# Convolution stretches and bias tables in other steps of an input projection

## The chip, the cores and the metric

The kernel runs on one core of one Trainium2 chip. The metric is the device time of one execution in microseconds (us). TensorE (PE) multiplies matrices and transposes, VectorE (DVE) and ScalarE (ACT) work on tiles in SBUF and PSUM, GpSimd (POOL) on tiles in SBUF, and SyncE (SP) issues nearly all transfers.

## The reference, cut to what matters

One block of a diffusion backbone on 2048 latent and 256 context tokens of 1024 channels, all in float32. The part that the change touches is the input projection and what is made from its output:

```python
hx = modulate(rms_norm(x, norm1_g[i]), sh1, sc1)
qx, kx, vx, ux = split_proj(hx @ w_in[i])          # 512 + 512 + 512 + 1024 columns
qx_rot = axial_rope(qx, row_pos, col_pos)
kx_rot = axial_rope(kx, row_pos, col_pos)
attn_x = neighbourhood_attention(qx_rot, qx, kx_rot, vx, kc, vc, rpb[i])   # bias from rpb
conv_x = conformer_conv(ux, ...)                   # a * sigmoid(b), width 31, LayerNorm, silu
x_new = x + g1 * (jnp.concatenate([attn_x, conv_x], axis=-1) @ w_out[i])   # then the MLP
```

The vectors sh1, sc1, g1, ... come from `silu(c) @ w_ada + b_ada`.

## The kernel before, in words

Every float32 product is made of three matmuls on a high and a low part of each operand (mm3, L89 to L92). The program runs through a start, the input projection (56 to 665 us), attention, the output projection and the MLP; only the input projection is touched.

**Steps.** The 2048 tokens are two blocks of 1024, each of two halves of 512. For each block there are ten groups of 256 columns of the weight: four gated groups (u), two q, two k and two v. A step is one group on one half, 40 steps in all: block 0 has steps 0 to 19 (u 0 to 7, q 8 to 11, k 12 to 15, v 16 to 19), block 1 steps 20 to 39 in the same manner. Within a group the halves follow each other, but the first two u groups of a block are interleaved, as are the v groups of block 1. In each step TensorE fills one piece of PSUM (pt); ScalarE, VectorE and GpSimd then make what is stored: h_d from u (sg, L724 and L725), rotated and split q and k (rope_store, L576 on, with products by the cosine and sine tables), v (L613 on).

**PSUM.** It is cut into four pieces of 1024 columns, given out in turn by psA (L54). During the input projection the convolution holds one of them (pcv, L416), so three rotate.

**Convolution.** It goes in 21 stretches of 98 rows (class Conv): load (cw from h_d, L425), split (ScalarE L428, VectorE L429), fwd (three matmuls into pcv, the product cy on VectorE at L435, its high part cyh on ScalarE at L438, the low part cyl on VectorE at L439), inv one step later (six matmuls, LayerNorm on VectorE, L448 to L452) and turn another step later (four transposes L458, ScalarE L460, store L462). cy is a tile in SBUF. A counter, cv_pos, says which stretch stands where: the stretches start with the last u step of a block and one enters per step, in steps 7 to 16 and 27 to 37. The load of the next stretch is issued at the end of a step.

**Beside it.** norm_half scales the four x tiles of a half on VectorE (L218) and shifts them on GpSimd (L221). The relative-position bias is built in four parts: bias_start and bias_end (step 6), bias_head (steps 8 to 15; tables tb, a mask add on GpSimd at L287, stores to tf_d and ti_d), and bias_rows (groups 9 to 12; twelve DRAM-to-DRAM copies into bias_d, L304). ada_chunk makes the gate vectors from the weight rows wr (L490, L506); its finish (L511 on) does two matmuls (L514), loads the row of b_ada (br, L517) and adds it (L518).

The order on each engine is that of a scheduler from these calls; the SP queue issues transfers in the order that `order` prints.

Of the kernel before, what the change touches and what calls it, by code (L numbers as in the profile page):

```python
# [18 lines left out]
P = 128  # L19
D = 1024  # L20
# [21 lines left out]
def hybrid_layer(ctx: ExitStack, tc: tile.TileContext, a: dict, out: bass.AP):  # L42
# [375 lines left out]
    class Conv:  # L418
# [12 lines left out]
        def fwd(self):  # L431
            i, hl, o = self.i, cvc["hl"], cvc["ps"][:, 0:512]
            mm3(o, hl[:, 0, 0:P], hl[:, 1, 0:P], self.w[:, 1, :], self.w[:, 0, :], True, True)
            y = pa.tile([P, 2, 512], F32, tag="acc", bufs=2, name=f"cy{i}")
            VE.tensor_tensor(y, o.unsqueeze(1).broadcast_to([P, 2, 512]), cvc["ab"], ALU.mult)  # L435
            self.yh = pa.tile([P, 2, 512], F32R, tag="H", bufs=3, name=f"cyh{i}")
            self.yl = pa.tile([P, 2, 512], F32R, tag="H", bufs=3, name=f"cyl{i}")
            SE.copy(self.yh, y)  # L438
            VE.tensor_tensor(self.yl, y, f(self.yh), ALU.subtract)  # L439
# [22 lines left out]
            SY.dma_start(cv_d[:, :, self.t0:self.t0 + self.n].rearrange("k p n -> p k n"), cx[:, :, 0:self.n])  # L462

    cvs = [Conv(i) for i in range(NCB)]
    cv_pos = [0]

    def conv_at(d, last):
        i = cv_pos[0] - d  # L470
        if 0 <= i < last and not hasattr(cvs[i], f"did{d}"):
            setattr(cvs[i], f"did{d}", True)
            (Conv.inv, Conv.turn)[d - 1](cvs[i])

    def conv_end(last):
        i = cv_pos[0]
        if i < last:
            cvs[i].split()
            cvs[i].fwd()
            if i + 1 < last:  # L480
                cvs[i + 1].load()
        cv_pos[0] += 1

    def ada_chunk(ch):
        box = {}

        def load(i):
            n, k = i // KD, i % KD
            r = pa.tile([P, 512], F32, tag="wr", bufs=2, name=f"wr{ch}_{i}")
            SY.dma_start(r, wada[k * P:(k + 1) * P, ch * D + n * 512:ch * D + (n + 1) * 512])  # L490
            box[i] = r

        def step(i):
            if i == 0:
                box["a"] = pa.tile([P, D], F32, tag="ada", bufs=1, name=f"ada{ch}")
                load(0)
                return
            if i < 2 * KD:
                load(i)
            r = box.pop(i - 1)  # L500
            n, k = (i - 1) // KD, (i - 1) % KD
            acc = box["a"][:, n * 512:(n + 1) * 512]
            if k == 0:
                VE.tensor_scalar(acc, r, sil[:, 0:1], None, ALU.mult)
            else:
                VE.scalar_tensor_tensor(acc, r, sil[:, k:k + 1], acc, ALU.mult, ALU.add)  # L506
            if i == 2 * KD:
                pe_todo.append(finish)

        def finish():  # L510
            acc = box["a"]  # L511
            pg = psA(f"pg{ch}")
            for n in range(2):
                TE.matmul(pg[0:1, n * 512:(n + 1) * 512], ones[:, 0:1], acc[:, n * 512:(n + 1) * 512],  # L514
                          start=True, stop=True)
            br = pa.tile([1, D], F32, tag="m1", bufs=2, name=f"br{ch}")
            SY.dma_start(br, a["b_ada"][:, ch * D:(ch + 1) * D])  # L517
            VE.tensor_tensor(br, pg[0:1, :], br, ALU.add)  # L518
            row = {2: 0, 4: 1, 3: 2}[ch]
            if ch == 4:  # L520
                gr = gtile([1, D], F32, "gr")
                SY.dma_start(gr, a["norm2_g"])
                VE.scalar_tensor_tensor(br, br, 1.0, gr, ALU.add, ALU.mult)
            SY.dma_start(g_d[row:row + 1, :], br)
        return [(0.6, lambda i=i: step(i)) for i in range(2 * KD + 1)]
# [19 lines left out]
    def norm_half(tiles, b, hf):  # L545
        scale, shift = norm_mod(tiles, Ar, Br, f"n{b}{hf}")
        for i in range(4):
            scale(i)
            shift(i)
        return tiles  # L550

    def trans_half(tiles, b, hf, which=range(4)):
# [124 lines left out]
    first_x(3)  # L677
    mix0 = Mix(0, lambda nm: gtile([P, 1024], F32, nm), None)
    NG = len(groups)
    CB0 = (BLK - P + PAD) // CL + 1  # L680
    CBS = (CB0, NCB)
    BR0 = 9
    adas = {ch: ada_chunk(ch) for ch in (2, 3, 4)}
    G0 = NG // NB
    ADA = {G0 - 1: 2, G0: 3, G0 + 2: 4}
    RATE = {"u": (5.2, 6), "q": (5.2, 4), "k": (5.2, 4), "v": (5.2, 6)}
    xt1 = xd = None
# [22 lines left out]
    def half(gi, hf):  # L710
        b, kind, idx, _ = groups[gi]
        wget = wgets[gi]
        thv, tlv = TH[hf] if TH[hf] else (None, None)
        if kind == "u":
            ct = idx
            pt = psA(f"pu{b}{ct}{hf}")
            for t in range(4):
                for k in range(KD):
                    wh, wl = wget(k, slice(0, 2 * P))
                    sl = slice(t * P, (t + 1) * P)  # L720
                    mm3(pt[:, t * 256:(t + 1) * 256], thv[:, k, sl], tlv[:, k, sl], wh, wl, k == 0, k == KD - 1)
            sg = gtile([P, 4, P], F32, f"sg{b}{ct}{hf}")
            p4 = pt.rearrange("p (t j c) -> p t j c", t=4, j=2)
            SE.activation(sg, p4[:, :, 1, :], AF.Sigmoid)  # L724
            VE.tensor_tensor(sg, p4[:, :, 0, :], sg, ALU.mult)  # L725
            t0 = PAD + b * BLK + hf * 512
            SY.dma_start(h_d[t0:t0 + 512, ct * P:(ct + 1) * P].rearrange("(t p) c -> p t c", p=P), sg)
            if ct == 3 and hf == 1:
                cv_pos[0] = (0, CB0)[b]
                cvs[cv_pos[0]].load()  # L730
                conv_end(CBS[b])
        elif kind in "qk":
            pt = psA(f"p{kind}{b}{idx}{hf}")
            for j in range(2):
                conv_at(2 - j, CBS[b])
                for k in range(KD):
                    lh, ll = wget(k, slice(j * P, (j + 1) * P))
                    mm3(pt[:, j * 512:(j + 1) * 512], lh, ll, thv[:, k, :], tlv[:, k, :], k == 0, k == KD - 1)
            rope_store(b, kind, idx, hf, pt)
            conv_end(CBS[b])  # L740
        else:
            for t2 in range(2):
                def getter(tt, thv=thv, tlv=tlv):
                    sl = slice(tt * P, (tt + 1) * P)
                    return lambda k: (thv[:, k, sl], tlv[:, k, sl])
                row = (b * BLK + hf * 512 + t2 * 256) // W
                conv_at(2 - t2, CBS[b])
                if idx == 1 and hf == 1 and b + 1 < NB:
                    trans_half(pend["x"], b + 1, 0, (2 * t2, 2 * t2 + 1))
                v_tiles([getter(2 * t2), getter(2 * t2 + 1)], row, wget, idx, f"{b}{idx}{hf}{t2}")  # L750
            conv_end(CBS[b])
        if gi == 1 and hf == 0:
            trans_half(xt1, 0, 1)
            in_order(n_start, (VE.engine, SE.engine, GE.engine))
        if kind == "v" and idx == 1 and b + 1 < NB and hf == 1:
            TH[1] = None
            pend["x"] = x_half(b + 1, 1)
        if b > 0 and kind == "u" and idx == 0 and hf == 0:
            norm_half(pend["x"], b, 1)
        if b + 1 < NB and kind == "q" and idx == 1 and hf == 0:  # L760
            norm_half(pend["x"], b + 1, 0)
        if b > 0 and kind == "u" and idx == 1 and hf == 0:
            trans_half(pend.pop("x"), b, 1)
        if gi == 0 and hf == 1:

            ts_ = []
            for i in range(2):
                xt = x_tile(f"xc{i}")
                SY.dma_start(xt, cin[i * P:(i + 1) * P, :])
                ts_.append(xt)  # L770
            scale, shift = norm_mod(ts_, Ac, Bc, "nc")
            for i in range(2):
                scale(i)
                shift(i)
                SY.dma_start(xc_d[i * P:(i + 1) * P, :], ts_[i])
        if gi == 3 and hf == 0:
            bias_start()
            bias_end()
        if 4 <= gi < 8:
            bias_head((gi - 4) * 2 + hf)  # L780
        if gi == 1 and hf == 1:
            conv_loads()
        if gi == 2 and hf == 1:
            conv_tables()
        if hf == 0 and BR0 <= gi < BR0 + 4:
            bias_rows(gi - BR0)
        todo, pe_todo[:] = list(pe_later), list(pe_todo)
        pe_later[:], pe_todo[:] = list(pe_todo), []
        for fn in todo:
            fn()  # L790
        if kind == "v" and idx == 1 and b + 1 < NB:
            pass
        else:
            pump(*RATE[kind])
# [61 lines left out]

    steps[-4:] = [(NG - 2, 0), (NG - 1, 0), (NG - 2, 1), (NG - 1, 1)]
    for i, (gi, hf) in enumerate(steps):

        for nxt, nh in steps[i + 1:i + 3]:  # L860
            if nh == 0 and nxt not in wgets and len(wgets) < 2:
# [747 lines left out]
```

## Time and profile before

| what | us |
|---|---|
| median of 3 runs | 2565.85 |
| lowest, highest | 2565.72, 2567.3 |
| profiled execution | 2570.69 |
| its span | 2568.9 |
| TensorE busy in the span | 2430.5 (95%) |
| VectorE, GpSimd, ScalarE busy | 1790.2, 1467.8, 1248.7 |

The rows in the section below come from the profiled execution. TensorE is the engine that is nearly always at work; a wait counts for the time where it makes TensorE stand still. A row of waits names the waiting engine and line, what it waited for, the sum in us, how often, and the longest one. The granted clock (PEclk) is a share of TensorE's full speed: 1.00 is 2.4 GHz, 0.50 is 1.2 GHz.

### The profile page before, as it was taken

To read this page: it belongs to the slowest core of one execution; us is meant where nothing else is said; L and a number is where in the kernel's file an instruction comes from. 1 tells how busy PE (TensorE), PEld (TensorE's weight loads), DVE (VectorE), ACT (ScalarE), POOL (GpSimd) and SP (SyncE) were. 2 spreads that over 40 slices of the span, in tenths; PEclk is the share of its full clock that TensorE was granted. 3 is DMA by queue.
4 is the path that set the end of the run, shared out by engine and by line. 5 is a ranking of instruction groups with operands and counts; after the bars stand their busy time and mean duration, and the time that the engine had idled before them with its cause. 6 is when DMAs were issued, how large, how long until landed. Compare 5 with 4: busy or idle time off the path is not lost.

```text
span 2568.9 us, 42313 instructions
## 1 busy us (share of the span) xinstructions
PE 2430.5 (95%) x15903; PEld 2216.9 (86%) x15903; DVE 1790.2 (70%) x2465; ACT 1248.7 (49%) x2162; POOL 1467.8 (57%) x1055
## 2 busy tenths in 40 slices
PE   7997989899889999988999999999999999999997
PEld 5985889689889999987998889999889998799996
DVE  6646743666689976468666697666786676876676
ACT  4334531443689963134444554444554445454442
POOL 3537422442578856457555676555675556755564
PEclk9998999999999999999999999999999999999999
DMA  8555764653899865665333443333343334433321
GB/s 299 158 168 163 223 216 130 196 154 110 227 253 262 241 182 174 195 231 165 99 99 107 129 139 111 101 105 99 121 148 101 99 99 126 137 107 100 105 92 57
DMA packets 293882, 387.26 MB, mean 151 GB/s; under 512 B 38021, under 2 KB 231228, under 8 KB 293644
## 3 DMA queue, kind: packets, MB, share of 16 engines
q1 hardware_dynamic: 293660, 384.54, 49.7%
q8 instruction: 125, 2.05, 0.3%
q14 instruction: 81, 0.66, 0.1%
q10 hardware_dynamic: 16, 0.00, 0.0%
HBM read 308.03 MB, written 86.76 MB: 154 GB/s over the span
## 4 chain that ended last, share of the span: by engine, by line
PE 62%; DVE 10%; DMA 9%; POOL 5%; issue 4%; SPq 2%; ACT 1%; DVEq 0%; POOLq 0%; ACTq 0%
PE pall L90 18%; PE pall L91 18%; PE pall L92 18%; PE pall L1105 2%; PE pall L1069 1%; PE pall L1030 1%; DVE s L1398 1%; DMA ar<-at_d 1%; DVE ac L1501 1%; DVE ac L1497 1%; PE pall L1107 1%; DVE w L1423 1%; PE pall L1032 1%; DMA cw<-h_d 1%; DMA xn_d<-xo 1%
## 5 line engine op out<-in xcount | busy, mean ns | idle before, releaser
L90 PE MATMUL pall<-w,hh 128*128 128x512 f32 x1024 | 406.0, 397 | 11.0 <-DVE ac L1497 7.2
L91 PE MATMUL pall<-w,hh 128*128 128x512 f32 x1024 | 403.0, 394 | 0.0
L92 PE MATMUL pall<-w,hl 128*128 128x512 f32 x1024 | 397.2, 392 | 0.6 <-DVE hl L1454 0.6
L1497 DVE TENSOR_TENSOR ac<-pall,ac 128x1024 f32<-128x1024 f32 x239 | 286.8, 1214 | 73.9 <-PE pall L92 73.2
L90 PEld LDWEIGHTS pall<-w,hh 128*128 128x128 f32 x1024 | 195.1, 190 | 51.6 <-issue 4.4
L92 PEld LDWEIGHTS pall<-w,hl 128*128 128x128 f32 x1024 | 193.3, 189 | 41.9 <-DVE hl L1454 2.2
L91 PEld LDWEIGHTS pall<-w,hh 128*128 128x128 f32 x1024 | 194.8, 190 | 36.4 <-issue 0.2
L1451 ACT ACTIVATE c<-c 128x512 f32<-128x512 f32 x128 | 80.9, 632 | 157.2 <-DVE c L1471 129.2
L86 POOL TENSOR_TENSOR w_0l<-w_0r,w_0h 128x1024 fp32r<-128x1024 f32 x20 | 50.7, 2537 | 172.7 <-ACT w_0h L85 152.5
L90 PE MATMUL pall<-xah,w 128*128 128x256 f32 x512 | 144.8, 284 | 4.7 <-ACT w L1392 4.7
L92 PE MATMUL pall<-xah,w 128*128 128x256 f32 x512 | 145.2, 284 | 0.0
L91 PE MATMUL pall<-xal,w 128*128 128x256 f32 x512 | 145.0, 283 | 0.0
L1454 DVE TENSOR_TENSOR hl<-c,hh 128x512 fp32r<-128x512 f32 x128 | 123.7, 967 | 15.3 <-ACT hh L1453 15.2
L1062 POOL TENSOR_SCALAR sb<-sb,ri 128x696 f32<-128x696 f32 (+1 forms) x128 | 105.6, 826 | 49.7 <-DVE ri L1057 40.7
L1044 DVE CUSTOM_DVE_ANT_0 sb<-pall,bias 128x696 f32<-128x696 f32 (+1 forms) x128 | 108.0, 845 | 6.5 <-PE pall L1032 5.9
L1052 ACT ACTIVATE sb<-sb,mn 128x696 f32<-128x696 f32 (+1 forms) x128 | 109.6, 857 | 0.6 <-DVE mn L1044 0.6
L90 PEld LDWEIGHTS pall<-xah,w 128*128 128x128 f32 x512 | 98.1, 192 | 7.5 <-ACT w L1392 4.9
L91 PEld LDWEIGHTS pall<-xal,w 128*128 128x128 f32 x512 | 98.6, 192 | 2.8
L92 PEld LDWEIGHTS pall<-xah,w 128*128 128x128 f32 x512 | 98.6, 192 | 2.1
L90 PE MATMUL pall<-xth,w 128*128 128x256 f32 x256 | 75.2, 294 | 19.1 <-DVE pu L1459 19.1
L1105 PE MATMUL pall<-pw,v 120*128 120x256 f32 (+1 forms) x480 | 90.8, 309 | 0.8 <-ACT ob L1112 0.8
L1081 DVE TENSOR_TENSOR pw<-pall,pw 120x512 fp32r<-120x512 f32 (+1 forms) x128 | 83.5, 653 | 5.1 <-ACT pw L1076 4.7
(853 smaller groups left out, 8797.0 us busy)
## 6 DMA issues: line engine op xcount, KB each, us to landing
v<-v_d SPq DMA_DIRECT2D x144, 120.0 KB
q<-q_d SPq DMA_DIRECT2D x64, 256.0 KB
wr<-in_w_ada SPq DMA_DIRECT2D x48, 256.0 KB
v_d<-vt SPq DMA_DIRECT2D x64, 160.0 KB
wa<-in_w_ada SPq DMA_DIRECT2D x8, 1024.0 KB
x<-in_x SPq DMA_DIRECT2D x16, 512.0 KB
kr<-k_d SPq DMA_DIRECT2D x32, 256.0 KB
at_d<-ao SPq DMA_DIRECT2D x32, 256.0 KB
```

The source lines that it names most:

```text
L86: (eng or GE).tensor_tensor(l, r, f(h), ALU.subtract)
L90: TE.matmul(outp, lh, rh, start=start, stop=False)
L91: TE.matmul(outp, lh, rl, start=False, stop=False)
L92: TE.matmul(outp, ll, rh, start=False, stop=stop)
L1044: VE.tensor_tensor_reduce(sb[:, c0:SE_], d["s"][:, 512 - SC0 + c0:768], bt[:, c0:SE_], -1.0, 3e38, ALU.add, ALU.min, mn)
L1052: SE.activation(pb[:, c0:SE_], pb[:, c0:SE_], AF.Exp, bias=d["mn"], scale=-1.0, accum_out=d["sm"])
L1062: GE.tensor_scalar(pb[:, c0:SE_], pb[:, c0:SE_], d["ri"], 1.0, ALU.mult, ALU.mult)
L1081: VE.tensor_tensor(pw[0:120, 0:nch, 1, :], d["tv"], f(pw)[0:120, 0:nch, 0, :], ALU.subtract)
L1105: TE.matmul(o, VT[(pr, *key)][0:n, hd, :], pw[0:n, ch, :, :], start=(ch == 0), stop=False)
L1451: SE.activation(c, c, AF.Relu)
L1454: VE.tensor_tensor(dl, cv, f(dh), ALU.subtract)
L1497: VE.tensor_tensor(ac, po_, ac, ALU.add)
```

## The change

A table, ENTER, now says which stretch enters at which step: 0 to 7 in steps 12 to 19, 8 and 9 in steps 22 and 24, and 10 to 20 in steps 27 to 37 as before. The u steps call conv_at too. cy lies in a rotating piece of PSUM instead of SBUF. bias_start and bias_end go to step 17, bias_head to steps 20 to 27, bias_rows to groups 14 to 17. The row of b_ada is loaded at the end of a chunk's steps instead of in finish, and of the last half's four x tiles two are shifted on VectorE.

```diff
-            y = pa.tile([P, 2, 512], F32, tag="acc", bufs=2, name=f"cy{i}")
+            y = psA(f"cy{i}").rearrange("p (z n) -> p z n", z=2)
...
-    def conv_at(d, last):
-        i = cv_pos[0] - d
-        if 0 <= i < last and not hasattr(cvs[i], f"did{d}"):
-            setattr(cvs[i], f"did{d}", True)
+    def conv_at(d):
+        i = ENTER.get(now[0] - d)
+        if i is not None:
             (Conv.inv, Conv.turn)[d - 1](cvs[i])
 
-    def conv_end(last):
-        i = cv_pos[0]
-        if i < last:
+    def conv_end():
+        i = ENTER.get(now[0])
+        if i is not None:
             cvs[i].split()
             cvs[i].fwd()
-            if i + 1 < last:
-                cvs[i + 1].load()
-        cv_pos[0] += 1
+        i = ENTER.get(now[0] + 1)
+        if i is not None:
+            cvs[i].load()
...
             if i == 2 * KD:
+                box["b"] = pa.tile([1, D], F32, tag="m1", bufs=2, name=f"br{ch}")
+                SY.dma_start(box["b"], a["b_ada"][:, ch * D:(ch + 1) * D])
                 pe_todo.append(finish)
...
-            br = pa.tile([1, D], F32, tag="m1", bufs=2, name=f"br{ch}")
-            SY.dma_start(br, a["b_ada"][:, ch * D:(ch + 1) * D])
+            br = box["b"]
...
-            shift(i)
+            shift(i, VE if b and hf and i % 2 else GE)
...
-    BR0 = 9
+    G0 = NG // NB
+    NS0 = 2 * G0
+
+    ENTER = {n: i for i, n in enumerate([*range(12, 20), 22, 24, *range(27, 38)])}
+    assert len(ENTER) == NCB
+    BR0 = G0 + 4
...
             for t in range(4):
+                if t % 2 == 0:
+                    conv_at(2 - t // 2)
...
-            if ct == 3 and hf == 1:
-                cv_pos[0] = (0, CB0)[b]
-                cvs[cv_pos[0]].load()
-                conv_end(CBS[b])
+            conv_end()
...
-        if gi == 3 and hf == 0:
+        if gi == G0 - 2 and hf == 1:
             bias_start()
             bias_end()
-        if 4 <= gi < 8:
-            bias_head((gi - 4) * 2 + hf)
+        if G0 <= gi < G0 + 4:
+            bias_head((gi - G0) * 2 + hf)
```

The three places on which the terms of the prediction rest, by the order of the instructions on an engine. First VectorE at the end of block 0's q steps and the start of its k steps, before (sw and m10 belong to the rotation, x are the first half's tiles of block 1, cy and cyl the convolution's):

```order
L585 STREAM_SHUFFLE sw0q_1883<-pall 128x1024
L594 TENSOR_TENSOR m10q_1884<-pall,cos_440 128x1024
L452 TENSOR_SCALAR co_1851<-co_1851,cst_1852 98x512
L218 SCALAR_TENSOR_TENSOR x_1645<-x_1645,n10ss,Ar 128x1024
...
L435 TENSOR_TENSOR cy_1922<-pall,cab 128x1024
L607 TENSOR_TENSOR ql0q_1888<-pall,qh0q_1887 128x256 x2
L439 TENSOR_TENSOR cyl_1925<-cy_1922,cyh_1924 128x1024
L585 STREAM_SHUFFLE sw0k_2022<-pall 128x1024
L588 SCALAR_TENSOR_TENSOR m10k_2023<-pall,cos_440 128x1024
```

and now:

```order
L585 STREAM_SHUFFLE sw0q_1706<-pall 128x1024
L594 TENSOR_TENSOR m10q_1707<-pall,cos_440 128x1024
L130 RECIPROCAL n10ss<-n10ss 128x4
L218 SCALAR_TENSOR_TENSOR x_1537<-x_1537,n10ss,Ar 128x1024
...
L607 TENSOR_TENSOR ql0q_1711<-pall,qh0q_1710 128x256 x2
L585 STREAM_SHUFFLE sw0k_1802<-pall 128x1024
L588 SCALAR_TENSOR_TENSOR m10k_1803<-pall,cos_440 128x1024
L435 TENSOR_TENSOR pall<-pall,cab 128x1024
L589 SCALAR_TENSOR_TENSOR sw0k_1802<-sw0k_1802,sin_441 128x1024
L439 TENSOR_TENSOR cyl_1817<-pall,cyh_1816 128x1024
```

The lines of the convolution (L452, L435, L439) are gone from beside the scales of the x tiles; the first stretch comes in the first k step, its product goes to pall (PSUM), and cyl reads it there.

SP where the copies into bias_d stand, before, in the v steps of block 0:

```order
L592 DMA k_d<-m10k_2338 128x512 x2
L635 DMA v_d<-vt_2436 40x2x512 x3
L304 DMA bias_d_81<-tf_d 16x32x320
L304 DMA bias_d_82<-ti_d 16x32x440
L304 DMA bias_d_83<-tf_d 16x32x320
L701 DMA sin_2985<-in_sin_t 128x1024
L425 DMA cw_2356<-h_d 128x512
...
L635 DMA v_d<-vt_2507 40x2x512 x4
...
L462 DMA cv_d<-ccx_2378 128x4x98
```

and now, in the second q step of block 1 (cw_4175 is the load of stretch 12; q_d takes the rotated q of the step before):

```order
L290 DMA tf_d<-tb_4019 32x600
L291 DMA ti_d<-tb_4019 32x320
L489 DMA wr_10_4030<-in_w_ada 128x512
L489 DMA wr_11_4033<-in_w_ada 128x512
L304 DMA bias_d_81<-tf_d 16x32x320
L304 DMA bias_d_82<-ti_d 16x32x440
L304 DMA bias_d_83<-tf_d 16x32x320
...
L489 DMA wr_12_4036<-in_w_ada 128x512
L425 DMA cw_4175<-h_d 128x512
L610 DMA q_d<-qh1q_4135 64x2x512 x2
```

At the "..." of the second piece stand nine more copies and nothing else; before, loads and stores stood between groups of two to four of them.

GpSimd at the second half's x tiles of block 1, before:

```order
L86 TENSOR_TENSOR w_1l<-w_1r,w_1h 128x1024
L221 TENSOR_TENSOR x_2962<-x_2962,Br 128x1024
L221 TENSOR_TENSOR x_2964<-x_2964,Br 128x1024
L221 TENSOR_TENSOR x_2966<-x_2966,Br 128x1024
L221 TENSOR_TENSOR x_2968<-x_2968,Br 128x1024
```

now:

```order
L86 TENSOR_TENSOR w_1l<-w_1r,w_1h 128x1024
L287 TENSOR_TENSOR tb_2948<-tb_2948,cm 64x600
L221 TENSOR_TENSOR x_2779<-x_2779,Br 128x1024
L221 TENSOR_TENSOR x_2783<-x_2783,Br 128x1024
L287 TENSOR_TENSOR tb_3137<-tb_3137,cm 64x600
```

and VectorE there now:

```order
L729 TENSOR_TENSOR sg_2925<-pall,sg_2925 128x512
L130 RECIPROCAL n11ss<-n11ss 128x4
L218 SCALAR_TENSOR_TENSOR x_2779<-x_2779,n11ss,Ar 128x1024
...
L218 SCALAR_TENSOR_TENSOR x_2785<-x_2785,n11ss,Ar 128x1024
L221 TENSOR_TENSOR x_2781<-x_2781,Br 128x1024
L729 TENSOR_TENSOR sg_3089<-pall,sg_3089 128x512
L221 TENSOR_TENSOR x_2785<-x_2785,Br 128x1024
L230 TENSOR_TENSOR t11l<-pall,t11h 128x8x128 x4
```

Two of the four adds of Br are on VectorE, around a product of a gated step (sg), and two table adds (L287) stand beside the other two on GpSimd.

## Rows read from the trace of the kernel before

**Rows 1.** Page, part 1: busy us, share of the span, instructions.

```profile
PE 2430.5 (95%) x15903; PEld 2216.9 (86%) x15903; DVE 1790.2 (70%) x2465; ACT 1248.7 (49%) x2162; POOL 1467.8 (57%) x1055
```

**Rows 2.** TensorE's waits, 150 to 400: us in total, times, longest.

```profile
PE pall L91 <- DVE cyl L439: 8.0, 2, 6.5
PE pall L227 <- POOL x L221: 6.3, 3, 2.8
PE pall L90 <- ACT cyh L438: 5.1, 1, 5.1
PE pall L90 <- ACT ccx L460: 3.3, 1, 3.3
PE pall L458 <- DVE cy L435: 2.3, 1, 2.3
PE pall L90 <- ACT cw L428: 1.8, 1, 1.8
...
```

**Rows 3.** Windows: us, PE busy, granted clock, DMA share, GB/s.

```profile
203.10:206.50 3.40, 3.40 (x9) 0.50 0.75 161
237.20:257.70 20.50, 8.90 (x21) 0.50 0.60 171
377.10:387.40 10.30, 8.02 (x37) 0.50 0.09 25
496.60:503.40 6.80, 3.73 (x9) 0.50 0.82 261
```

**Rows 4.** TensorE's waits, 440 to 660.

```profile
PE pall L90 <- DVE br L518: 5.3, 1, 5.3
PE pall L90 <- ACT ccx L460: 3.9, 2, 2.0
PE pall L91 <- DVE cyl L439: 2.4, 2, 1.2
PE pall L90 <- ACT cyh L438: 1.9, 2, 1.0
PE pall L458 <- DVE cy L435: 1.6, 1, 1.6
```

**Rows 5.** Lines L439 and L435: duration ns min/median/max, first and last start.

```profile
L439 DVE TENSOR_TENSOR cyl<-cy,cyh x21: 1206/1226/9344, 161.0 to 645.5; 128x1024 fp32r<-128x1024 f32 x21
...
L435 DVE TENSOR_TENSOR cy<-pall,cab x21: 1186/1211/1227, 158.7 to 643.2; 128x1024 f32<-128x1024 f32 x21
```

**Rows 6.** Timelines of VectorE and GpSimd, 236 to 254: start us, us.

```profile
242.54 9.34 DVE L439 TENSOR_TENSOR cyl<-cy,cyh 128x1024 fp32r<-128x1024 f32 x1 [5.82 <-ACT cyh L438]
...
240.18 9.27 POOL L221 TENSOR_TENSOR x<-x,Br 128x1024 f32<-128x1024 f32 x4
```

**Rows 7.** DMA issues, 300 to 340: count, KB each.

```profile
bias_d<-tf_d SPq DMA_DIRECT2D x8, 640.0 KB
bias_d<-ti_d SPq DMA_DIRECT2D x4, 880.0 KB
```

**Rows 8.** Window of the copies, columns as in rows 3.

```profile
301.80:337.00 35.20, 32.18 (x257) 1.00 0.99 321
```

**Rows 9.** Chain of waits, 295 to 345: start us, us.

```profile
305.57 9.86 DMA cw<-h_d
...
316.18 0.50 PE pall L90
```

**Rows 10.** Timeline of SP, 468 to 500.

```profile
472.75 11.01 SPq L490 DMA_DIRECT2D wr<-in_w_ada  x5
483.87 0.38 SPq L425 DMA_DIRECT2D cw<-h_d  x1
```

**Rows 11.** Timeline of TensorE, 487 to 500.5.

```profile
487.75 1.02 PE L514 MATMUL pall<-ada,ones 128*1 128x512 f32 x2
...
499.67 0.79 PE L90 MATMUL pall<-t11h,w_0h 128*128 128x512 f32 x1 [5.34 <-DVE br L518]
```

More of the change, by code (lines that the diff above doesn't have):

```diff
@@ L464, in hybrid_layer @@
     cvs = [Conv(i) for i in range(NCB)]
-    cv_pos = [0]
-    def conv_at(d, last):
-        i = cv_pos[0] - d
-        if 0 <= i < last and not hasattr(cvs[i], f"did{d}"):
-            setattr(cvs[i], f"did{d}", True)
+    now = [0]
+    def conv_at(d):
+        i = ENTER.get(now[0] - d)
+        if i is not None:
             (Conv.inv, Conv.turn)[d - 1](cvs[i])
-    def conv_end(last):
-        i = cv_pos[0]
-        if i < last:
+    def conv_end():
+        i = ENTER.get(now[0])
+        if i is not None:
             cvs[i].split()
             cvs[i].fwd()
-            if i + 1 < last:
-                cvs[i + 1].load()
-        cv_pos[0] += 1
+        i = ENTER.get(now[0] + 1)
+        if i is not None:
+            cvs[i].load()
     def ada_chunk(ch):
@@ L679, in hybrid_layer @@
     NG = len(groups)
-    CB0 = (BLK - P + PAD) // CL + 1
-    CBS = (CB0, NCB)
-    BR0 = 9
+    G0 = NG // NB
[3 more added lines that the diff above has]
+    BR0 = G0 + 4
     adas = {ch: ada_chunk(ch) for ch in (2, 3, 4)}
-    G0 = NG // NB
     ADA = {G0 - 1: 2, G0: 3, G0 + 2: 4}
@@ L734, in half @@
             for j in range(2):
-                conv_at(2 - j, CBS[b])
+                conv_at(2 - j)
                 for k in range(KD):
@@ L739, in half @@
             rope_store(b, kind, idx, hf, pt)
-            conv_end(CBS[b])
+            conv_end()
         else:
@@ L746, in half @@
                 row = (b * BLK + hf * 512 + t2 * 256) // W
-                conv_at(2 - t2, CBS[b])
+                conv_at(2 - t2)
                 if idx == 1 and hf == 1 and b + 1 < NB:
@@ L750, in half @@
                 v_tiles([getter(2 * t2), getter(2 * t2 + 1)], row, wget, idx, f"{b}{idx}{hf}{t2}")
-            conv_end(CBS[b])
+            conv_end()
         if gi == 1 and hf == 0:
@@ L858, in hybrid_layer @@
     for i, (gi, hf) in enumerate(steps):
+        now[0] = i
         for nxt, nh in steps[i + 1:i + 3]:
```

## The prediction, made before the changed kernel had run

> **What bounds the kernel now.** I read the page's busy shares first, then what TensorE waits for in each stretch, then its granted clock there, then the other engines' instructions at those moments. TensorE is busy for 95% of the span [rows 1], so a change in the input projection pays only where TensorE stands still or runs at half its clock. The first thing to see is that the second half of block 0, where its convolution stretches run today, has such places: six kinds of waits between 150 and 400 us, 8.0 + 6.3 + 5.1 + 3.3 + 2.3 + 1.8 = 26.8 us [rows 2]. The second is the clock: in three pieces next to these waits the granted clock is 0.50, the lower of the two levels (1.2 instead of 2.4 GHz), after TensorE had stood waiting. Work there takes twice as long, so half of TensorE's busy time in them is lost: (3.40 + 8.90 + 8.02) / 2 = 10.2 us [rows 3]. Block 0 thus loses 37.0 us around its stretches. Block 1 loses less: 5.3 + 3.9 + 2.4 + 1.9 + 1.6 = 15.1 us of waits [rows 4], and 3.73 / 2 = 1.9 us to one half-clock piece [rows 3].
>
> The third thing is why the worst waits are there. The low half of the split spectrum (cyl, L439) reads two tiles in SBUF and takes 1.226 us as a rule but once 9.344 us, while the product before it (cy, L435), which reads PSUM and one SBUF tile, never takes more than 1.227 us [rows 5]. The 9.34 us one starts at 242.54 and ends at 251.88; four adds of GpSimd (L221), reading SBUF too, run from 240.18 to 249.45, and TensorE waits for it meanwhile [rows 6]. Two engines that want two SBUF operands each do not run side by side here.
>
> **The change part by part.** My sum is made against the profiled execution, 2570.69 us (span 2568.9 and 1.8 around it). It lies 4.84 us above the median of the runs, 2565.85 us; I apply the difference to the median.
>
> *Block 0's stretches leave the q and u steps for k, v and the first u steps of block 1, and cy goes to PSUM.* The order shows the q steps with nothing of the convolution between L594 and the scales of the next x tiles, and cyl reading PSUM. So the four adds of L221 no longer hold cyl (6.5 of the 8.0 us), the chains behind it vanish (cyh 5.1, ccx 3.3, cy 2.3, cw 1.8), and with the idle time goes most of the half clock (10.2). What stays: the second half's x tiles of block 1 still arrive late, one wait of the longest kind now, 2.8 us [rows 2]; a wait for a stretch's load or transposition in a v step, about the 1.8 and 0.4 now, taken as 2.2. So 37.0 - 2.8 - 2.2 = 32.0 us gained; bounds 27 (two more waits of 2.3) and 36.
>
> The same work is added to k, v and u steps at the prices it has now, 1.21 us for L435 and 1.23 us for L439 [rows 5], beside matrix work that does not read its result until the next step. I cost it at nothing as long as VectorE is not late when the next tile in PSUM is asked for.
>
> The rule of the Trainium skill, "SBUF — State Buffer", section "Who interferes with whom", that a VectorE instruction with two SBUF inputs contends with a GpSimd one that reads SBUF, while one with a single SBUF input does not, agrees with the trace (9.344 us against at most 1.227 us). It speaks against one detail: two of the four shifts of block 1's second half now run on VectorE with two SBUF inputs, beside adds of GpSimd; if each lost an add of 9.27 / 4 = 2.3 us, the gain would be 4.6 us smaller.
>
> *The relative-position tables move to block 1.* The order shows all twelve DRAM-to-DRAM copies (L304) in one row on SP, behind the load wr 11 and ahead of wr 12, of the stretch load cw12 and of the q stores. Before, they stand in four groups with a sine table, a stretch load and v stores between them. Eight of 640 KB and four of 880 KB [rows 7] are 8.85 MB. At 301.8 to 337, where they run today, the DMA share is 0.99 at 321 GB/s [rows 8], so they take 27.6 us. There a stretch load of 256 KB issued behind three copies and the sine table (3.0 MB with itself, 9.3 us at that rate) needed 9.86 us to land [rows 9]: a load waits for what stands ahead of it. Now cw12: SP issues five wr loads from 472.75 over 11.01 us and cw12 at 483.87 [rows 10]. Taking the first of the five as wr 11, a turn of 11.01 / 5 = 2.2 us puts the copies at 475.0 (on the clock of before; everything earlier moves together). They drain at 475.0 + 27.6 = 502.6; wr 12 and cw12, 0.52 MB, at 504.2; the split and the first matmul follow 0.75 us after landing (316.18 - 305.57 - 9.86) [rows 9], at 504.9. TensorE reaches that matmul at 487.75 + 1.02 = 488.8, behind the two matmuls of the gate vector [rows 11]. So a new stall of 504.9 - 488.8 = **16.1 us**; bounds 13.9 (copies from 472.75) and 26 (copies from 478, at the 261 GB/s of the 496.6 piece [rows 3]).
>
> Behind this stall VectorE and ScalarE come late once more for the next stage of the same stretch. Such waits now cost 2.3 (cy) to 5.1 us (cyh) [rows 2]; I take the middle, 3.7. After so long a stop TensorE runs at half clock for a piece like those now: 1.9 to 4.45 us [rows 3]; I take 3.0. Taken off is what stands in that place today: the 5.34 us for the bias row [rows 11], whose load is now issued earlier, one ccx wait of 2.0 that falls into the new stall [rows 4], and the half-clock 1.9. Net of this part: 16.1 + 3.7 + 3.0 - 5.3 - 2.0 - 1.9 = **+13.6 us**.
>
> *Block 1's u steps* now carry the table loads and stores on SP, the mask adds on GpSimd, and stretches 7 to 9. The trace shows no u step with a stretch in it. From below nothing, if all lies beside matrix work; from above two waits of the kind ccx has, 6.6; I take one, 3.3, less a little for the wide u tiles: +3.0.
>
> *cy in PSUM for block 1* takes away one of the two cyl waits: -1.2 [rows 4].
>
> Sum: -32.0 + 13.6 + 3.0 - 1.2 = **-16.6 us**, so 2549.3 us by the median, 2554.1 for an execution like the profiled one. Adding the terms' bounds as independent (downwards 4, 5 and 3; upwards 5, 13 and 4) gives 2542 to 2564 for this case.
>
> **Rivals.** *The copies do not hold TensorE.* cw12 could land while the copies still run, since they are many small pieces on engines that it shares. Then the whole new stall is away and the old 5.3 and 1.9 too: -32.0 - 7.2 + 3.0 - 1.2 = -37.4, 2528.5 us. Against it stands the 9.86 us of the load that had 2.7 MB ahead of it [rows 9]. The Trainium skill, "DMA: Bandwidth & Descriptors", section "Queues, rings and completion order", says that completion is not first in, first out per issuing engine; no row here shows a load that overtook the copies. Chance 0.10.
>
> *Slower: the drain is long.* Place and price: the copies start only where SP issues cw12 today, 483.87, because they wait for the last table's stores, and drain at the lowest rate per busy share in rows 3, 161 / 0.75 = 215 GB/s, in 41.2 us; with 2.4 for the two loads and 0.75 TensorE starts at 528.2, a stall of 39.4 instead of 16.1: -16.6 + 23.3 = +6.7, 2572.5 us. It decides from a drain that ends 16.6 us later than mine, at 519.2. For it: small rows of 1.3 KB and one row of twelve copies; against it: the 321 GB/s were measured on these same copies. Chance 0.10.
>
> *The waits only move.* cy now takes a rotating piece of PSUM that the steps' own tiles need, from L435 to the end of cyl, at least 1.21 + 1.23 us. Were each of the 21 stretches to hold the next tile by 0.95 us, 20 of the 32 us come back: +3.4, 2569.3 us. It decides from 16.6 / 21 = 0.8 us each. Against it: the order puts a whole step between cy and the tile that takes its place. Chance 0.10.
>
> **How the numbers follow.** Forecast 0.70 at 2549.3; the rivals 0.10 each. About 0.2% (5.1 us) is what a measurement of this kernel can tell from no change, so faster means under 2560.7. The forecast's own range leaves some 0.07 of its 0.70 above that; with the first rival and a little of the third, faster has 0.75. Same: 0.06 of the forecast, 0.07 of the third and 0.01 of the second, 0.14. Slower: 0.11. The range runs from 2535 (towards the first rival, where the stall is half gone) to 2566 (towards the third): 2 in 10 lie outside, the first rival below, the second and part of the third above.
>
> **What would show it.** In the profile after: TensorE's waits for cyl, cyh and cw in 150 to 400 near nothing, and no half-clock piece in the q steps; cyl never far over 1.3 us; twelve copies issued in one row in the second q step of block 1, DMA share near 0.99 for some 28 us, and one wait of TensorE for cw of about 16 us behind it with half clock after. Wrong if that wait is missing or over 30 us, if the u steps of block 1 show more than 7 us of new waits, or if block 0 keeps over 10 us of its own.

## The result: slower by 0.74%

The changed kernel takes 2585.63 us (median of four runs, 2581.84 to 2588.03), the kernel before 2566.18 us in the same comparison. The ratio is 1.0074, 95% interval 1.0056 to 1.0091. I had forecast 2549.3 us and a range from 2535 to 2566. The profiled execution of the changed kernel took 2581.84 us (span 2580.1), the lowest of its four; the profiled one of before took 2570.69, more than any of the four runs that its median comes from. So the two traces differ by 11.2 us, while the medians differ by 19.5: some 8 us of the loss lie in differences between executions and are not in these traces.

To see where the time went, I cut both traces at the same work: the starts of the first q step of block 0 (step 8), of block 1's first u step (20), its first q step (28), its first v step (36), and the end of the projection. The first view is that of windows with these borders; columns: us, TensorE busy, granted clock, DMA share, GB/s. Before:

```profile
158.50:348.78 190.28, 168.08 (x929) 0.94 0.68 200
348.78:459.63 110.85, 104.55 (x813) 0.95 0.46 138
459.63:603.03 143.40, 131.01 (x649) 0.98 0.53 163
603.03:665.28 62.25, 59.40 (x474) 1.00 0.47 140
```

and the changed kernel:

```profile
155.08:324.00 168.92, 157.25 (x892) 0.98 0.60 178
324.00:443.07 119.07, 110.41 (x852) 0.97 0.47 133
443.07:617.46 174.39, 139.36 (x653) 0.88 0.62 190
617.46:677.96 60.50, 58.85 (x471) 1.00 0.46 139
```

The durations alone mislead, since the change moves matrix work between these pieces (the u steps of block 1 hold 27 matmuls and 16 transposes of the convolution now, 3 matmuls before). So I count TensorE's **loss**: the time without a matmul, plus half of the matmul time at the lower of the two clocks, 1.2 GHz, both summed over the trace's intervals.

| loss of TensorE, us | before | changed |
|---|---|---|
| block 0: q, k, v (steps 8 to 19) | 28.4 | 13.2 |
| block 1: u (20 to 27) | 10.3 | 10.7 |
| block 1: q, k (28 to 35) | 14.3 | 44.3 |
| block 1: v (36 to 39) | 2.9 | 1.7 |
| sum | 55.8 | 69.8 |

The sum is 14.0 us more. To come from there to the 11.2, take off 3.4 us that this execution was ahead at step 8 and 1.5 less behind the borders, and add 2.1 more of matrix work between them. Nothing is read from the 3.4: other runs below with the same instructions up to step 8 reach it up to 3 us later.

What TensorE waits for in the changed kernel, 150 to 400 us, the four largest rows (of the same form as [rows 2]):

```profile
PE pall L90 <- DVE ql0q L607: 7.6, 1, 7.6
PE pall L227 <- DVE x L221: 4.5, 1, 4.5
PE pall L227 <- POOL x L221: 1.5, 1, 1.5
PE pall L90 <- ACT cw L428: 1.5, 1, 1.5
```

and 440 to 660 us, where [rows 4] stood, the four largest:

```profile
PE pall L90 <- ACT cw L428: 19.0, 1, 19.0
PE pall L458 <- DVE pall L435: 7.5, 4, 2.4
PE pall L90 <- ACT cyh L438: 3.8, 1, 3.8
PE pall L812 <- DMA xd<-xc_d: 3.5, 1, 3.5
```

Its half-clock pieces, in windows as in [rows 3]:

```profile
214.30:221.10 6.80, 3.08 (x7) 0.50 0.21 45
354.30:361.10 6.80, 4.02 (x19) 0.50 0.25 74
453.30:456.70 3.40, 2.83 (x7) 0.51 0.97 298
480.60:507.90 27.30, 8.47 (x20) 0.50 1.02 335
521.50:531.80 10.30, 7.28 (x22) 0.50 0.72 205
```

Two things stand out. In block 0 the waits for cyl and cyh are gone, as intended, but a new one of 7.6 us for the last read of a q step's tile has come. In block 1 one wait for a stretch load is 19.0 us, with a whole train of waits and half clock around it.

**The row of copies** can be read from SP's timeline of the changed kernel (start, us of issue):

```profile
462.31 0.55 SPq L304 DMA_DIRECT2D bias_d<-tf_d  x1
...
480.26 2.18 SPq L304 DMA_DIRECT2D bias_d<-tf_d  x1
482.54 2.23 SPq L489 DMA_DIRECT2D wr<-in_w_ada  x1
484.88 0.55 SPq L425 DMA_DIRECT2D cw<-h_d  x1
```

The window until the stretch load lands, with the columns of the windows above:

```profile
462.30:495.00 32.70, 13.38 (x58) 0.78 0.99 317
```

And TensorE's next matmul in its timeline, with what it waited for in brackets:

```profile
495.71 0.80 PE L90 MATMUL pall<-cw,chl 128*128 128x512 f32 x1 [19.02 <-ACT cw L428]
```

The queue drains at 317 GB/s with a DMA share of 0.99, from 462.3 to about 495, and TensorE has stood since 476.7.

**The scales.** VectorE's timeline at 205 to 218 us shows what the last read, L607, stood behind:

```profile
205.86 11.77 DVE L218 SCALAR_TENSOR_TENSOR x<-x,n10ss,Ar 128x1024 f32<-128x1024 f32 x4
217.55 0.74 DVE L607 TENSOR_TENSOR ql0q<-pall,qh0q 128x256 fp32r<-128x256 f32 x2
```

GpSimd's timeline there:

```profile
206.61 3.38 POOL L598 TENSOR_TENSOR m10q<-m10q,sw0q 128x1024 f32<-128x1024 f32 x1
209.95 9.92 POOL L221 TENSOR_TENSOR x<-x,Br 128x1024 f32<-128x1024 f32 x3
```

TensorE's:

```profile
218.02 0.79 PE L90 MATMUL pall<-t01h,w_0h 128*128 128x512 f32 x1 [7.65 <-DVE ql0q L607]
```

Four scales took 11.77 us. In the kernel before they took 4.86. VectorE's and GpSimd's timelines there:

```profile
229.41 4.86 DVE L218 SCALAR_TENSOR_TENSOR x<-x,n10ss,Ar 128x1024 f32<-128x1024 f32 x4
229.16 6.42 POOL L287 TENSOR_TENSOR tb<-tb,cm 64x600 f32<-64x600 f32 x1
```

There GpSimd's table add L287, 1.46 us at the least, was the one that was held, until the scales were through; the adds of the shift came behind them and hit cyl [rows 6]. Now GpSimd's rotation add and shift adds stand beside the scales, and the two engines take turns: three of the four scales took 3.4 us each instead of 1.27, and GpSimd's adds 3.3 to 3.4 instead of 2.3 to 2.4.

### The profile page after: what moved, and what is told of

Its sections match the earlier page's. It is cut to its first block, busy times and chain, and to the rows that moved or that the text cites. A ratio compares the mean times of both kernels' runs of the same rounds, so it can differ in the third digit from the quotient of the medians.

```text
span 2580.1 us, 42309 instructions
## 1 busy us (share of the span) xinstructions
PE 2434.9 (94%) x15903; PEld 2220.3 (86%) x15903; DVE 1785.1 (69%) x2467; ACT 1261.3 (49%) x2172; POOL 1458.3 (57%) x1053
## 4 chain that ended last, share of the span: by engine, by line
PE 67%; DVE 9%; DMA 7%; POOL 3%; issue 3%; SPq 1%; ACT 1%; DVEq 0%; ACTq 0%; POOLq 0%
PE pall L90 20%; PE pall L91 19%; PE pall L92 19%; PE pall L1107 2%; PE pall L1071 2%; PE pall L1032 2%; DMA wr<-in_w_ada 1%; DVE s L1400 1%; DVE ac L1503 1%; PE pall L1109 1%; PE pall L1034 1%; PE pall L1091 1%; DVE ac L1499 1%; DVE w L1425 1%; SPq L304 1%
## 5 line engine op out<-in xcount | busy, mean ns | idle before, releaser
L86 POOL TENSOR_TENSOR w_0l<-w_0r,w_0h 128x1024 fp32r<-128x1024 f32 x20 | 50.1, 2506 | 144.1 <-ACT w_0h L85 133.1
L90 PE MATMUL pall<-xth,w 128*128 128x256 f32 x256 | 75.3, 294 | 16.6 <-DVE pu L1461 16.6
L505 DVE SCALAR_TENSOR_TENSOR ada<-wr,sil,ada 128x512 f32<-128x512 f32 x42 | 52.0, 1238 | 52.5 <-DMA wr<-in_w_ada 51.8
```

What stands on the lines that cost most here:

```text
L90: TE.matmul(outp, lh, rh, start=start, stop=False)
```

## The experiments

Times are medians, and each ratio is to the kernel before on the same chip. In these runs the kernel before took 2570 to 2572 us, 2566 in the comparison above; so ratios are to be compared, not times. The changed kernel has 1.0074 from the comparison above; it was not run again beside these.

**Tables back in block 0.**

```diff
-    BR0 = G0 + 4
+    BR0 = 9
...
-        if gi == G0 - 2 and hf == 1:
+        if gi == 3 and hf == 0:
             bias_start()
             bias_end()
-        if G0 <= gi < G0 + 4:
-            bias_head((gi - G0) * 2 + hf)
+        if 4 <= gi < 8:
+            bias_head((gi - 4) * 2 + hf)
```

> The changed kernel with the relative-position tables and the twelve copies back at their old steps in block 0; stretches, cy in PSUM and the shifts as changed. Theory A (the row of twelve copies in block 1 is the largest loss: between the starts of steps 28 and 36 TensorE needs 174 us instead of 143): that stretch comes back to 143 to 150 us, the time falls by 20 to 30 us against the changed kernel, to 2555 to 2566, less what the copies cost the stretches that now stand beside them in block 0's k and v steps (up to 10). Theory B (the stretches in other steps and cy in PSUM are the loss, the copies only lie where the wait shows): block 1's q steps still need over 160 us, the time stays at 2578 or more.

Measured 2586.64 us, ratio 1.0058 (1.0040 to 1.0076). The time is theory B's, the place is A's: steps 28 to 35 need 143.6 us, with 14.8 of loss, as before. But block 0 and the u steps together lose 58.3 us instead of 23.9, far over the 10 that A allowed: block 0 loses 37.1 instead of 13.2, and block 1's u steps 21.2 instead of 10.7. (The profiled execution is the slowest of seven, 8 us above their median, but it needs 1910.2 us behind the projection, where the changed kernel's trace has 1901.6.) The wait for L607 behind the scales, which take 13.62 us here, grows to 18.5:

```profile
PE pall L90 <- DVE ql0q L607: 18.5, 1, 18.5
```

So the two moves hang together: with the stretches in the k and v steps, the tables in block 0 go with 34 us more of loss up to step 28 (24 in block 0 itself), about what they cost block 1 in one row (30 more).

**cy in SBUF.**

```diff
-            y = psA(f"cy{i}").rearrange("p (z n) -> p z n", z=2)
+            y = pa.tile([P, 2, 512], F32, tag="acc", bufs=2, name=f"cy{i}")
```

> The changed kernel with cy back in an SBUF tile. Theory A (cy takes one of three rotating pieces of PSUM, so a step's tile reuses the piece of two steps before instead of three, and the second k step of block 0 waits 7.6 us for the last read, L607, behind the four scales of x): the 7.6 us wait and the half clock behind it (3.4) vanish, some waits for cyl and cyh of 1 to 2 us return; time lower by 5 to 11 us, 2575 to 2581. Theory B (TensorE waits because VectorE is late with everything behind the scales, whichever tile it is): about the same wait under another name, 2582 to 2590.

Measured 2582.57 us, ratio 1.0044 (1.0029 to 1.0060), some 8 us under the changed kernel by the ratios, but the two intervals overlap. In the trace each theory has a part. There is no wait for L607 any more, though the scales are as long (11.87 us); TensorE starts the second k step at once (A). But it waits 4.4 us a little later under another name, for cyh (B):

```profile
226.41 0.75 PE L90 MATMUL pall<-cyh,chl 128*98 128x512 f32 x1 [4.37 <-ACT cyh L438]
```

Block 0 loses 8.8 us instead of 13.2. Thus the lost piece of rotation turned VectorE's lateness into 3 us more of a wait; the lateness itself is the scales'. What I had not looked for: with the row of copies as it was, and the same stall of 19.0 us, steps 28 to 35 lose 35.8 us instead of 44.3, with 0.7 for xd instead of 3.5. So cy's place may have a share in what follows the stall too. The u steps lose 22.6 instead of 10.7 in this execution, 7.1 of it in a wait for L452 (see the last section), and no run separates these.

**All four shifts of the second half on GpSimd.**

```diff
-            shift(i, VE if b and hf and i % 2 else GE)
+            shift(i)
```

> The changed kernel with all four shifts of block 1's second half on GpSimd again. Theory A (VectorE's two shifts with two SBUF inputs stand in each other's way with GpSimd's adds: the scales took 6.98 us, the shifts 3.35 and 1.88, and TensorE waited 4.5 + 1.5 us and ran at half clock for 6.8): the waits for x fall to 2 to 4 us, time lower by 2 to 5, 2581 to 2584. Theory B (four adds of 2.3 to 3.3 us behind a table add on GpSimd are as late as the two on VectorE): no change within 2 us of 2585.6, or some us slower.

Measured 2588.15 us, ratio 1.0064 (1.0041 to 1.0086): not to be told from the changed kernel. TensorE waits 5.9 us for x in three pieces instead of 4.5 + 1.5 in two; loss in the u steps 12.9 against 10.7. Theory B. This detail of the change neither helps nor hurts.

**Copies spread.**

```diff
-    BR0 = G0 + 4
+    COPY = (28, 29, 30, 31, 31, 32, 33, 33, 34, 35, 35, 36)
...
-        if hf == 0 and BR0 <= gi < BR0 + 4:
-            bias_rows(gi - BR0)
+        if now[0] in COPY:
...
+            for n in range(COPY.count(now[0])):
+                bias_copy(copies.popleft())
...
```

The lines left out pin each copy on SP behind the stretch load that was issued last.

> The changed kernel with the twelve copies pinned on SP, one or two behind the stretch load of each of the steps 28 to 36, instead of in one row. Theory A (a stretch load waits for everything ahead of it on the queue; one copy ahead costs 640 or 880 KB, 2 to 2.8 us, and TensorE has that much slack): the 19.0 us wait and what follows it (waits for L435, for the context tile and half clock) go, steps 28 to 36 need 145 to 152 us instead of 174, time 2557 to 2566. Theory B (these steps have no room for 8.85 MB more, however it is spread: the q stores need the queue as well): the waits come in small pieces, steps 28 to 36 need over 160 us, time over 2572.

Measured 2566.68 us, ratio 0.9978 (0.9963 to 0.9994). Theory A: the ratio is 0.0096 under the changed kernel, some 25 us; the 2566.68 itself lies just above A's 2557 to 2566, but the kernel before, too, ran some 5 us longer here. Steps 28 to 35 need 151.3 us and lose 22.0 instead of 44.3. What TensorE waits for between 440 and 600 us no longer has cw in it; the three largest rows (in kernels with spread copies the lines stand some rows further down: L443 is cyh, L510 the gate's sum, L828 or L834 the context tile, L457 the line L452):

```profile
PE pall L90 <- ACT cyh L443: 7.6, 2, 3.8
PE pall L520 <- DVE ada L510: 2.9, 1, 2.9
PE pall L90 <- DVE ct L828: 2.9, 1, 2.9
```

The same 8.85 MB fit into these steps without a wait for a stretch load. It is their place on the queue that costs, not their bytes.

**Without the four adds of the first half.**

```diff
-            shift(i, VE if b and hf and i % 2 else GE)
+            if not (b == 1 and hf == 0):
+                shift(i, VE if b and hf and i % 2 else GE)
```

> The changed kernel without the four shift adds (L221) of the first half of block 1's x tiles on GpSimd; what it leaves out is the addition of the shift vector to those 512 tokens, so its time is not that of the whole computation. It is for one look at VectorE's four scales (L218) there, 11.77 us in the changed kernel and 5.1 us in the one before, with GpSimd's rotation, weight-low and shift adds beside them. Theory A (the scales, which read two SBUF tiles, wait for GpSimd's adds): with the adds gone the four scales take 6 to 9 us, the wait of the second k step for L607 falls from 7.6 to 2 to 5 us. Theory B (something else makes the scales long: the weight split alone, or their own operands): still 11 to 12 us and 7 to 8 us of wait.

One execution, 2586.18 us. The scales are shorter, in VectorE's timeline:

```profile
207.78 8.55 DVE L218 SCALAR_TENSOR_TENSOR x<-x,n10ss,Ar 128x1024 f32<-128x1024 f32 x4
216.25 0.74 DVE L608 TENSOR_TENSOR ql0q<-pall,qh0q 128x256 fp32r<-128x256 f32 x2
```

and so is TensorE's wait (L608 is the line L607):

```profile
216.72 0.80 PE L90 MATMUL pall<-t01h,w_0h 128*128 128x512 f32 x1 [4.40 <-DVE ql0q L608]
```

Theory A: 3.2 us of the scales (11.77 to 8.55) and 3.25 of the wait are those adds. The other 3.7 over 4.86 stand beside GpSimd's work on the weights (L86) and the rotation, which still runs.

**The kernel before with cy in PSUM alone.**

```diff
-            y = pa.tile([P, 2, 512], F32, tag="acc", bufs=2, name=f"cy{i}")
+            y = psA(f"cy{i}").rearrange("p (z n) -> p z n", z=2)
```

> The kernel before with one part of the change alone: cy in a rotating piece of PSUM. Theory A (cyl no longer reads two SBUF tiles, so the 9.34 us cyl and the waits behind it, 6.5 and 5.1 us and half the half-clock stretch, go, but the steps' tiles lose one piece of rotation): cyl at most 1.3 us; some of the gain is given back as waits for the last read of a step's tile (L607) of a few us in the q steps; time 3 to 12 us under the kernel before. Theory B (the lost rotation costs as much as the lock): within 3 us of the kernel before or slower, with waits for L607 or L589 of 8 us and more in the q and k steps.

Measured 2574.92 us, ratio 1.0013 (0.9999 to 1.0027): theory B in the time, but mostly not by its mechanism. cyl is flat now, at most 1.232 us over the 21. Nevertheless TensorE waits 10.1 us in the same place, for cy, since VectorE is held at another instruction, the normalisation of the stretch before (L452, 0.55 us as a rule). VectorE's timeline:

```profile
225.86 6.05 DVE L452 TENSOR_SCALAR co<-co,cst 98x512 f32<-98x512 f32 x1
```

GpSimd's beside it:

```profile
225.53 1.46 POOL L287 TENSOR_TENSOR tb<-tb,cm 64x600 f32<-64x600 f32 x1 [1.00 <-DMA tb<-z_d]
226.96 2.37 POOL L86 TENSOR_TENSOR w_1l<-w_1r,w_1h 128x1024 fp32r<-128x1024 f32 x1
229.29 2.33 POOL L598 TENSOR_TENSOR m10q<-m10q,sw0q 128x1024 f32<-128x1024 f32 x1
```

and TensorE's:

```profile
238.55 0.42 PE L458 MATMUL pall<-ident,co 98*128 98x98 f32 x1 [10.13 <-DVE pall L435]
```

L452 ends (231.91) just after the third of GpSimd's instructions in a row (231.62). In block 1 a wait of the kind that B named has come, for the last read of a q tile, where TensorE waited 5.3 us for br before [rows 4]; VectorE is late there with the add of br (L518):

```profile
PE pall L811 <- DVE ql1q L607: 7.5, 1, 7.5
```

**One scale per step, copies spread.**

```diff
         if b + 1 < NB and kind == "q" and idx == 1 and hf == 0:
-            norm_half(pend["x"], b + 1, 0)
+            pend["n"] = norm_mod(pend["x"], Ar, Br, f"n{b + 1}{0}")
+        if now[0] in (12, 13, 14, 15):
...
+            pend["n"][0]((12, 13, 14, 15).index(now[0]))
...
+            pend["n"][1]((12, 13, 14, 15).index(now[0]))
```

The first call is the scale, pinned by the lines left out behind what VectorE has last, the step's cyl; the second is its shift.

> The changed kernel with the copies spread as in the run before (one or two behind each stretch load of steps 28 to 36) and the four scales of block 1's first half pinned one per step behind cyl of steps 12 to 15, each followed by its shift, instead of four in a row in front of L607. Theory A (the row of four scales beside GpSimd's adds is what the second k step waits for): that wait of 7.6 us and its half clock (1.6) go; 0 to 3 us come back as single scales beside GpSimd's adds; time 6 to 9 us under the spread copies alone, ratio to the kernel before about 0.995. Theory B (scales in the k steps delay cyl and the split of the next stretch there by as much): ratio 0.997 to 1.000.

Measured 2560.6 us, ratio 0.9960 (0.9944 to 0.9976). The interval overlaps that of the spread copies alone, and the 6 to 9 us of theory A came as some 5, between the two forecasts. In the trace the wait for L607 is gone and so is every half-clock piece of block 0: its loss is 6.5 us against 11.8. The u steps lost more in this execution (19.0 against 12.1, with a wait of 6.6 for L457, the line of L452), and it is the slowest of the six, so this profile can't split the gain further.

**The row of copies, later.** Against the spread copies:

```diff
-    COPY = (28, 29, 30, 31, 31, 32, 33, 33, 34, 35, 35, 36)
+    COPY = (30, 30, 30, 30, 30, 30, 30, 30, 30, 30, 30, 30)
```

> The changed kernel with the twelve copies still in one row, but pinned behind the load of the stretch that enters in step 31, so after the last weight rows of the gate vector and after all but the last q stores. Theory A (the row costs one stall of about its drain less one step, wherever it lies; the second round of waits in the changed kernel, 3.5 us for the context tile xd, 3.5 for L435 and 3.6 of half clock near 520 us, comes from the gate's weight rows wr 12 to 15 behind the copies): a wait for cw of 12 to 19 us at the next stretch, no wait for xd over 1 us, loss of TensorE between the starts of steps 28 and 36 of 30 to 38 us (44.3 in the changed kernel, 22.0 with the copies spread). Theory B (the row hurts only where q stores and weight rows need the queue): a wait for cw under 8 us, loss under 26 us, as good as spread.

Measured 2574.78 us, ratio 1.0025 (1.0013 to 1.0036). Neither theory: the wait for cw is 4.4 us, below A's, the loss in steps 28 to 35 is 26.7, above B's and below A's, and the time is not as good as spread. SP's timeline says why:

```profile
506.44 0.56 SPq L305 DMA_DIRECT2D bias_d<-tf_d  x1
...
517.59 2.44 SPq L305 DMA_DIRECT2D bias_d<-tf_d  x3
...
526.32 11.71 SPq L305 DMA_DIRECT2D bias_d<-tf_d  x4
...
540.18 1.57 SPq L429 DMA_DIRECT2D cw<-h_d  x1
```

Here the row, eleven copies from 517.6 after one at 506.4, starts 29 us before TensorE reaches the next stretch (547.0); in the changed kernel it was 14.4 us (462.3 to 476.7). So the wait is what the drain has left over at that moment: 32.7 - 14.4 = 18.3 us in the changed kernel and, for a drain as long, 32.7 - 29.4 = 3.3 here; with 0.7 for the split that is 19.0 and 4.0, against 19.0 and 4.4 measured. "One step" was the wrong size for the lead. There is no wait for xd, as A had it. That agrees with the second round of waits near 520 us coming from the gate: in the changed kernel xd, which takes the buffer of the gate's sum, is issued at 519.36, behind the gate's last matmuls at 518.3; before, at 494.98.

**Copies spread, two steps later, one scale per step.** Against the run with one scale per step:

```diff
-    COPY = (28, 29, 30, 31, 31, 32, 33, 33, 34, 35, 35, 36)
+    COPY = (30, 31, 32, 32, 33, 33, 34, 34, 35, 35, 36, 36)
```

> The kernel with spread copies and one scale per step, but the copies begin two steps later: one or two behind each stretch load of steps 30 to 36, none in steps 28 and 29, where the gate's weight rows and most q stores are issued. Theory A (what still goes wrong in steps 28 to 30, 3.0 us for the gate's sum, 3.8 for cyh, 1.2 for cyl and some 4 us of half clock, comes from the copies there): these go, loss between the starts of steps 28 and 36 falls from 18 to 22 us to 12 to 16, ratio to the kernel before 0.993 to 0.995. Theory B (two copies per step are too many in the k steps, or the waits in steps 28 to 30 have another cause): ratio 0.996 to 0.999.

Measured 2557.28 us, ratio 0.9952 (0.9935 to 0.9970): the best of all, faster than both kernels by its interval, though not told apart from the run with the earlier copies. The ratio lies between the two forecasts. The loss in steps 28 to 35 is 17.4 against 18.3, and the waits that A blamed on the copies are still there, here the three largest:

```profile
PE pall L90 <- ACT cyh L443: 4.3, 1, 4.3
PE pall L90 <- DVE ct L834: 2.9, 1, 2.9
PE pall L520 <- DVE ada L510: 2.7, 1, 2.7
```

So B in this: those three have another cause, which no run isolates.

## Why the prediction was wrong

**The gain up to step 28 was halved, for the most part by a step that I left out.** I took 37.0 us of loss and left 5.0, for late x tiles and stretch loads. Together with the u steps (+3.0) that was 29.0 us less. Measured is 38.7 to 23.9, 14.8 less (the 38.7 have two rows more than my 37.0, 1.7 us). Of the 14.2 us that are missing, 7.65 + 3.08 / 2 = 9.2 are the wait for L607 and its half clock in block 0. The step that failed is "I cost it at nothing as long as VectorE is not late", with the sentence that the four adds "no longer hold cyl". They do not, but VectorE is late all the same: GpSimd's instructions hold others of VectorE. The four scales, which stand in the order just ahead of these adds, I never priced with GpSimd beside them. Shown: without the adds the wait falls from 7.65 to 4.40; with the scales apart it is gone; and in the kernel before, cy in PSUM alone brings nothing, since L452 is held there instead of cyl.

**The other 5 us are x tiles that stay late.** All of the 10.3 us that block 1's u steps lost before are the waits for x, 6.3, and their half clock, 8.02 / 2 [rows 2 and 3]. My 32.0 of gain had most of this in it: one wait of 2.8 was to stay, and no half clock. Left are 4.5 + 1.5 = 6.0 us of waits and 4.02 / 2 = 2.0 of half clock. I gave no reason why two of the three waits should go, and the run with all four shifts on GpSimd has 5.9 us of the same waits.

**cy's place in PSUM** I costed at nothing too. My rival "the waits only move" named the right place, a tile that wants the piece that cy has taken, but gave it 0.10, because a whole step lies between. A whole step was not enough when four scales kept VectorE for 12 us: 7.65 us with cy in PSUM, 4.37 a little later with cy in SBUF.

**The stall behind the copies was right, what follows it was not.** Predicted 16.1 us from a drain of 27.6 at 321 GB/s; measured 19.0 at 317 GB/s. The term was short by 2.9, mostly traffic that I had left out of the drain: 10.4 MB ran in those 32.7 us and my sum had 9.4; the first q stores, issued from 485.52, run before the load has landed. Behind it: the next stage of that stretch 3.6 (2.36 + 1.24) against 3.7, half clock around it 8.47 / 2 = 4.2 in the piece from 480.6 against 3.0 (my range for it began at 1.9; [rows 3] have 3.40 / 2 = 1.7). What I did not see at all is the second round: 3.5 us for xd, 3.5 in two more waits for L435 and 7.28 / 2 = 3.6 of half clock near 525. I had asked only what stands behind the copies on the way to the next stretch, not that the gate's weight rows stand there too, and with them the buffer that xd needs. And 3.8 for cyh with 2.83 / 2 = 1.4 of half clock came in step 28, where 1.0 and 1.2 had been. That wait ended at 453.87, before the first copy was issued, so it is not the row's; its cause is open. Net +30.0 instead of +13.6.

**The two smaller terms.** New waits in the u steps were put at 3.0 us, and 2.7 came in the profiled execution (2.0 for L452, 0.7 for cyh and cyl). But other kernels with the same instructions there lost 12 to 19 us in all, where this one lost 10.7, so the point is not settled. Block 1's v steps gave 1.2, as forecast. Of the signs of being wrong that I had named, one came: block 0 keeps 13.2 us of its own, over 10.

**The rule on VectorE and GpSimd**, which I weighed for the two shifts only, held for instructions that I did not weigh: the scales, 3.4 us each in place of 1.27. For the shifts it was worth nothing measurable.

**The slower rival** had the right sign, 2572.5, by the wrong mechanism (a slow drain). I gave 0.11 to slower. Its decision point, a drain that ends 16.6 us later, was never reached; the loss came from what the stall set off and from the gain that was not there.

## What to carry to other kernels

When one instruction no longer waits for another engine, price the instructions that stay beside that engine as if each were the next victim: here the wait went only when one of the two bursts was taken apart (one scale per step). A row of transfers on one queue costs its drain less the lead before the first consumer; list every transfer behind it, and for each the buffer that it frees, and spread the row behind the loads that are waited for. And a tile that joins a rotation takes one piece of slack from all the others, which showed here in the steps where their last reader was late.

## What the hardware showed that I had not expected

VectorE can lose to GpSimd several times in a row: L452 with 6.05 us stood through three instructions of GpSimd, and in the kernel before one cyl of 9.34 through the last three of four adds [rows 6]. GpSimd can lose in the same way: its L287 took 6.42 us there, until VectorE's four scales were through. And in the changed kernel the two took turns, scale by add. Which of the three patterns comes is not explained by these runs.

L452 has one tile in SBUF and two columns of scalars, not two tiles, and took 6.05 and 6.32 us in one run where 0.55 is its rule. My sentence that two operands in SBUF are needed was thus too narrow, and the rule as I quoted it left out an exception. The Trainium skill, "SBUF — State Buffer", section "Who interferes with whom", says that a tensor_scalar can enter a mode of two ports and can then contend with GpSimd; the two long rows agree with it.

The waits at one place differ between executions of nearly the same program: the wait for L452 in block 1's u steps is 2.0 us in the profile of the changed kernel and about that in two of the others, and 6.6 to 7.2 in five. The traces show what differs. In the run with one scale per step two of VectorE's products for the gate (L510, two tiles in SBUF, 0.75 us as a rule) took 2.31 and 2.72 us and the line L452 behind them 1.48, beside GpSimd's work on the weights (L86, 2.41 and 2.34) and a table add (L287, 1.44). In the changed kernel the products and L452 came through in 0.74, 1.20 and 0.55, and L86 took 3.19 and 2.56. It is the same contest, won by the other side; what decides the order in one execution was not found.
